# Mixer A's output products in another order: all products with the maps, then all with the states, the two heads in turn

## The chip, the cores and the metric

The kernel runs on one core of a Trainium2 chip. The time is the device time of one execution in microseconds (us). TensorE multiplies matrices and writes to PSUM, which has 8 banks of 512 fp32 columns over 128 partitions; VectorE, ScalarE and GpSimd do the element-wise work (GpSimd has no part in the copies out of PSUM here), and the DMA engines bring the weights.

## The reference, cut to what matters

Two blocks run one after the other: a block of two layers with four mixers each, side by side, then a second block with gating, convolutions, sparse attention and an MLP. The change is in mixer A of the first block, a gated linear recurrence in two directions over 512 latent and 256 context tokens, with four heads of 64 dimensions:

```python
# S_t = diag(f_t) S_{t-1} + k_t^T v_t ; o_t = q_t S_t, in chunks
o_inter = jnp.einsum('bthk,bhkv->bthv', qf * jnp.exp(bcum), s)
diff = bcum[:, :, None] - bcum[:, None, :]
decay = jnp.exp(jnp.where(incl[None, :, :, None, None], diff, -jnp.inf))
att = jnp.einsum('bthk,bshk,btshk->bhts', qf, kf, decay)
o_intra = jnp.einsum('bhts,bshv->bthv', att, vf)
```

The output of a chunk is the sum of a product with the chunk's own map (`o_intra`, in this kernel one map for both directions together) and of a product with the state that enters the chunk (`o_inter`), one for each direction. Everything is fp32.

## The kernel before, in words

The whole program is unrolled by Python. Activities are generators: "fillers" (the projections with weights, which come in a fixed list) and side chains (mixer A, the attentions, the norms). A planner runs them against estimated times, always takes the next activity whose inputs its estimate calls ready, and so writes the program's order. It also picks an engine for many copies, by the estimated time at which ScalarE, VectorE or GpSimd comes free (`best`, used by `cp` and `ts`). Behind it, the framework orders the instructions of each engine once more and sets the waits, so the order that runs can differ in places from the order written.

Mixer A is `j_a(pair)`, called by `chain_a` for the two pairs of heads of a layer, one after the other. Tokens stand in chunks of 128: six in layer 0 (with context, in parts of four and two, `aparts`), four in layer 1 (one part). For a pair, `j_a` builds the maps `att` in seven levels (`level_mm`, VectorE's predicated copies), transposes the keys, computes the update of each chunk and direction (tile `up`) and runs the recurrence over the chunks into the states `S` (tile `si`, VectorE; forward the last chunk's state is chunk 3's, backward chunk 0's).

The output products stand in the last loop of `j_a` (lines 1552 to 1566). For each part it takes two PSUM banks, `ps`. Head `j` of the pair (0 or 1) owns bank `j` and in it partitions 64j to 64j+63; chunk c of the part owns 128 columns. For each chunk and head there are three products into the same columns: values times map (`va`, `att`: 128 rows of the array, 64 columns, line 1560), and for each direction `d` state times queries (`S`, `QZ`: rows and columns 64j to 64j+63, so head 0 sits in one quarter of the array and head 1 in the opposite one, line 1562). The first of the three has `start=True`, the last `stop=True`. Then the two banks are copied to the tile `y` (shown as `hn` in the trace), half by half (line 1565), with `cp("*", ...)`, which picks the engine. Behind that stand the square, the head norm (`co_headnorm`) and the gate.

In the planner's estimate (`time`, line 550) a product with `va` costs 135 ns and one with `S` half of that, 67.5.

In the trace an fp32 product of this kind is two MATMUL records, each with a LDWEIGHTS record (engine PEld).

The softmax attentions end in products of the same shape as those with `va` (`seg_bd`: 128 rows, 64 columns, 128 queries, tile `bdv`), in which the two heads take turns.

Of the kernel before, what the change touches and what calls it, by code (L numbers as in the profile page):

```python
# [18 lines left out]
D, S, CL = 1024, 512, 256  # L19
# [438 lines left out]
class K:  # L458
# [1035 lines left out]
    def j_a(self, pair):  # L1494

        nc, M, P = self.nc, self.M, self.P
        nq = self.nq
        qs, F = self.fq.pop(pair)
        KZ, QZ, TZ = M.new([128, 2, NT], tag="kh"), M.new([128, 2, nq], tag="qh"), M.new([128, 2, NT], tag="T")
        att, ks = M.new([128, 2, nq], tag="att"), M.new([128, nq], tag="ks")  # L1500
        for d in range(2):
            self.ts("*", KZ[:, d], F[:, d], -1.0, 1.0, ALU.mult, ALU.add)
            self.mul("*", QZ[:, d], qs.f, F[:, d, :nq])
        self.add("*", ks.f, KZ[:, 0, :nq], KZ[:, 1, :nq])
        at = lambda z: lambda c: z[:, c * 128:(c + 1) * 128]
        for c0, n in self.aparts():
            yield (ks, qs, self.bank(2))
            self.level_mm(at(ks), at(qs), att, None, c0, n)
        M.free(ks, qs)
        for i in range(7):  # L1510
            h = 1 << i
            yield (KZ,)
            ks = M.new([128, nq], tag="ks")
            self.cp("*", ks.rearrange("p (b w h) -> p b w h", w=2, h=h), self.aview(KZ, False, h, 0, nq))
            for c0, n in self.aparts():
                yield (QZ, ks, self.bank(2))
                self.level_mm(at(ks), lambda c: self.aview(QZ, True, h, c * 128, 128), att, i, c0, n)
            M.free(ks)
            Tc, o = (F, 0) if i == 0 else (TZ, NT - 2 * (NT >> i))
            o2 = NT - 2 * (NT >> (i + 1))  # L1520
            nt = NT >> (i + 1)
            for z, flip, n in ((QZ, True, nq), (KZ, False, NT)):
                v = self.aview(z, flip, h, 0, n)
                self.mul("*", v, v, self.tview(Tc, flip, o, n // (2 * h), h))
            Tv = Tc[:, :, o:o + 2 * nt].rearrange("p d (b w) -> p d b w", w=2)
            self.mul("*", TZ[:, :, o2:o2 + nt], Tv[:, :, :, 0], Tv[:, :, :, 1])
        o = NT - 2 * (NT >> 7)
        S = M.new([128, 2, 6, 64], tag="si")
        for d in range(2):
            yield (KZ, self.bank(2))  # L1530
            ps = self.new_bank(2)
            for c in range(6):
                nc.tensor.transpose(ps[:, c * 128:(c + 1) * 128], KZ[:, d, c * 128:(c + 1) * 128], self.ident.f)
            self.cp("*", F[:, d], ps[:, :NT])
            P.free(ps)
        M.free(KZ)
        for d, order in ((0, (4, 5, 0, 1, 2, 3)), (1, (5, 4, 3, 2, 1, 0))):
            yield (F[:, d], self.bank())
            up = self.new_bank()
            for c in range(6):  # L1540
                for j in range(2):
                    hh = 2 * pair + j
                    nc.tensor.matmul(up[64 * j:64 * j + 64, c * 64:(c + 1) * 64], F[:, d, c * 128 + 64 * j:c * 128 + 64 * j + 64],
                                     self.va[:, c, hh * 64:hh * 64 + 64], start=True, stop=True)
            yield (up[:, 0:384],)
            nc.gpsimd.memset(S[:, d, order[0]], 0.0)
            for a, b in zip(order[:-1], order[1:]):
                self.stt(S[:, d, b], S[:, d, a], TZ[:, d, o + a:o + a + 1], up[:, a * 64:(a + 1) * 64], ALU.mult, ALU.add)
            P.free(up)
        M.free(F, TZ)  # L1550
        y = M.new([128, nq], tag="hn")
        for c0, n in self.aparts():
            yield (S, QZ, att, self.bank(2))
            ps = self.new_bank(2)
            for c in range(c0, c0 + n):
                for j in range(2):
                    hh, r = 2 * pair + j, slice(64 * j, 64 * j + 64)
                    cc = slice(c * 128, (c + 1) * 128)
                    out = ps[r, j * 512 + (c - c0) * 128:j * 512 + (c - c0 + 1) * 128]
                    nc.tensor.matmul(out, self.va[:, c, hh * 64:hh * 64 + 64], att[:, j, cc], start=True, stop=False)  # L1560
                    for d in range(2):
                        nc.tensor.matmul(out, S[r, d, c], QZ[r, d, cc], start=False, stop=d == 1)
            for j in range(2):
                r = slice(64 * j, 64 * j + 64)
                self.cp("*", y[r, c0 * 128:(c0 + n) * 128], ps[r, j * 512:j * 512 + n * 128])
            P.free(ps)
        M.free(S, QZ, att)
        if pair == 1:
            M.free(self.va)
        yield (y,)  # L1570
        q = M.new([128, nq], tag="hq")
        self.act(q.f, y.f, AF.Square)
        self.spawn("hn", self.co_headnorm(y, q, self.V(f"hg{self.l}"), pair, 4e-6), 0)
# [952 lines left out]
```

## Time and profile before

| | us |
|---|---|
| median of 3 runs (1985.46 to 1990.9) | 1987.78 |
| the profiled execution | 1988.87 |
| its span, first to last instruction | 1987.1 |
| TensorE busy in it | 1871.8 |
| VectorE, ScalarE, GpSimd busy | 1199.5, 623.6, 527.4 |

The profile is that of one execution. "Busy" is the time in which an engine had at least one instruction under way; matmuls are pipelined, so two of them that overlap count once, and a busy TensorE is not one at its peak. A group's row gives start, busy time and count; the time that a group occupies is read from its start to the next group's start. "Idle before <- X" is the engine's idle time ahead of the instruction and what ended it; "issue" is time in which it waited for nothing that the profile shows.

### The profile page before, as it was taken

Reading aid. Unit: us, or ns where it says so; the run is one execution under the profiler, and the core shown is the slowest. Engines: PE = TensorE matmul, PEld = TensorE weight load, DVE = VectorE, ACT = ScalarE, POOL = GpSimd, SP = SyncE. Lnnn points to the kernel's source line nnn. Section 1 sums busy time; section 2 is a strip of 40 time slices with the busy share of each in tenths; the row PEclk is TensorE's granted clock in tenths of the full one; section 3 lists DMA queues with packets and bytes.
Section 4 is the critical chain, followed back from the end, with each engine's and each line's share of the span. In section 5 each row is a group of like instructions: output and inputs, shape, how many; then the busy total and the mean of one; then the engine's idle time right before and its main releaser. Section 6 shows DMA issues by size and latency. Waiting matters only on the chain.

```text
span 1987.1 us, 28567 instructions
## 1 busy us (share of the span) xinstructions
PE 1871.8 (94%) x11446; PEld 1542.3 (78%) x11446; DVE 1199.5 (60%) x2053; ACT 623.6 (31%) x1277; POOL 527.4 (27%) x453
## 2 busy tenths in 40 slices
PE   6899999899999999899999989989999999999999
PEld 4688677688877787776787777878788778888887
DVE  2657774655657738766556978774533655545542
ACT  2345444334630135444435231244423211000100
POOL 1314332532222414533133354421211320000000
PEclk9999989999999999999999999999999999999999
DMA  9100410200132401002214231211223322232221
GB/s 355 54 22 30 150 56 30 79 23 22 56 114 94 146 11 44 22 12 96 65 59 145 93 104 64 67 51 51 93 88 111 106 75 85 96 126 78 72 96 64
DMA packets 45380, 159.22 MB, mean 80 GB/s; under 512 B 5040, under 2 KB 5552, under 8 KB 44992
## 3 DMA queue, kind: packets, MB, share of 16 engines
q1 hardware_dynamic: 42224, 148.54, 21.9%
q10 hardware_dynamic: 3024, 8.85, 1.3%
q8 instruction: 90, 1.47, 0.3%
q14 instruction: 42, 0.34, 0.1%
HBM read 152.12 MB, written 5.26 MB: 79 GB/s over the span
## 4 chain that ended last, share of the span: by engine, by line
PE 40%; DVE 13%; issue 4%; POOL 4%; ACT 1%; DMA 1%; ACTq 0%; POOLq 0%; DVEq 0%; SPq 0%
PE banks L282 40%; DVE cacc L282 3%; POOL t L282 2%; DVE t L282 1%; DVE wlo L282 1%; DVE sm L282 1%; DVE z L282 1%; DVE p L282 1%; DVE h L282 1%; ACT p L282 1%; DVE whi L282 0%; DVE gt L282 0%; DVE xr L282 0%; POOL p L282 0%; POOL qh L282 0%
## 5 line engine op out<-in xcount | busy, mean ns | idle before, releaser
L282 PE MATMUL banks<-h,whi 128*128 128x512 f32 (+1 forms) x1968 | 579.1, 378 | 6.2 <-ACT h L282 2.8
L282 PEld LDWEIGHTS banks<-h,whi 128*128 128x128 f32 x1968 | 351.7, 190 | 66.9 <-ACT h L282 3.3
L282 PE MATMUL banks<-h,wlo 128*128 128x512 f32 (+1 forms) x984 | 366.5, 372 | 0.0
L282 PE MATMUL banks<-whi,h 128*128 128x256 f32 (+3 forms) x1344 | 335.8, 332 | 15.9 <-DVE h L282 7.9
L282 DVE TENSOR_TENSOR wlo<-raw,whi 128x1024 fp32r<-128x1024 f32 (+2 forms) x175 | 222.6, 1275 | 106.2 <-PE banks L282 59.7
L282 PEld LDWEIGHTS banks<-whi,h 128*128 128x128 f32 x1344 | 234.7, 192 | 42.3 <-DVE h L282 9.8
L282 PE MATMUL banks<-wlo,h 128*128 128x256 f32 (+3 forms) x672 | 219.8, 328 | 7.1 <-DVE wlo L282 6.0
L282 POOL TENSOR_TENSOR wlo<-raw,whi 128x1024 fp32r<-128x1024 f32 (+2 forms) x41 | 104.0, 2540 | 456.5 <-DMA out<-z 299.7
L282 PEld LDWEIGHTS banks<-h,wlo 128*128 128x128 f32 x984 | 186.6, 190 | 32.7 <-DVE wlo L282 0.4
L282 DVE TENSOR_REDUCE sm<-banks 128x1 f32<-128x768 f32 (+5 forms) x192 | 140.0, 750 | 56.1 <-PE banks L282 53.2
L282 ACT ACTIVATE p<-banks,sm 128x768 f32<-128x768 f32 (+5 forms) x192 | 141.6, 741 | 95.0 <-DVE sm L282 84.2
L282 ACT CAST whi<-raw 128x1024 fp32r<-128x1024 f32 (+2 forms) x88 | 88.3, 1007 | 223.3 <-PE banks L282 147.4
L282 PE MATMUL banks<-whi,hid 128*128 128x512 f32 x512 | 157.9, 389 | 0.0
L282 DVE CAST whi<-raw 128x1024 fp32r<-128x1024 f32 (+2 forms) x103 | 73.2, 715 | 116.0 <-PE banks L282 98.0
L282 PEld LDWEIGHTS banks<-wlo,h 128*128 128x128 f32 x672 | 129.0, 192 | 18.2 <-DVE wlo L282 7.5
L282 PEld LDWEIGHTS banks<-whi,hid 128*128 128x128 f32 x512 | 96.1, 188 | 19.8
L282 PE MATMUL banks<-ident,p 128*128 128x128 f32 x656 | 98.3, 282 | 12.2 <-POOL p L282 2.7
L282 ACT COPY p<-banks 128x768 f32<-128x768 f32 (+5 forms) x118 | 73.6, 630 | 99.1 <-PE banks L282 96.3
L282 POOL TENSOR_TENSOR t<-t,mhalf 128x1 f32<-128x1 f32 (+5 forms) x51 | 65.3, 1283 | 142.3 <-DVE t L282 136.5
L282 PEld LDWEIGHTS banks<-ident,p 128*128 128x128 f32 x656 | 75.6, 144 | 32.7 <-issue 7.7
L282 PE MATMUL banks<-wlo,hid 128*128 128x512 f32 x256 | 99.6, 389 | 0.0
L282 ACT ACTIVATE rl<-banks 128x512 f32<-128x512 f32 (+1 forms) x35 | 19.7, 562 | 169.2 <-PE banks L282 169.2
(334 smaller groups left out, 3003.9 us busy)
## 6 DMA issues: line engine op xcount, KB each, us to landing
raw<-wm SPq DMA_DIRECT2D x64, 512.0 KB, 3.5
raw<-win SPq DMA_DIRECT2D x60, 512.0 KB, 3.6
raw<-wada SPq DMA_DIRECT2D x48, 512.0 KB, 4.1
raw<-wgate SPq DMA_DIRECT2D x32, 512.0 KB, 3.5
raw<-wout SPq DMA_DIRECT2D x24, 512.0 KB, 3.5
raw<-w2f SPq DMA_DIRECT2D x10, 512.0 KB, 3.5
xr<-xtok SPq DMA_DIRECT2D x6, 512.0 KB, 6.2
x<-z SPq DMA_DIRECT2D x6, 512.0 KB, 2.6
```

Of the source, the lines that this page charges most:

```text
L282: return f(*a, **kw)
```

## The change

The three products of a chunk and head no longer stand together. For a part, first all products with the maps are written, over chunks and in each chunk over the two heads; then all products with the forward states in the same order; then all with the backward states. So neighbouring products always belong to different heads. Since a bank's sums now stay open until the last direction, `start` is set only on the first chunk's map product of each bank, and `stop` only on the last chunk's backward product. Tiles, operands, copies and the number of products stay.

```diff
-            for c in range(c0, c0 + n):
-                for j in range(2):
-                    hh, r = 2 * pair + j, slice(64 * j, 64 * j + 64)
-                    cc = slice(c * 128, (c + 1) * 128)
-                    out = ps[r, j * 512 + (c - c0) * 128:j * 512 + (c - c0 + 1) * 128]
-                    nc.tensor.matmul(out, self.va[:, c, hh * 64:hh * 64 + 64], att[:, j, cc], start=True, stop=False)
-                    for d in range(2):
-                        nc.tensor.matmul(out, S[r, d, c], QZ[r, d, cc], start=False, stop=d == 1)
+            cj = [(c, slice(c * 128, (c + 1) * 128), j, slice(64 * j, 64 * j + 64)) for c in range(c0, c0 + n) for j in range(2)]
+            out = lambda c, j: ps[64 * j:64 * j + 64, j * 512 + (c - c0) * 128:j * 512 + (c - c0 + 1) * 128]
+            for c, cc, j, r in cj:
+                hh = 2 * pair + j
+                nc.tensor.matmul(out(c, j), self.va[:, c, hh * 64:hh * 64 + 64], att[:, j, cc], start=c == c0, stop=False)
+            for d in range(2):
+                for c, cc, j, r in cj:
+                    nc.tensor.matmul(out(c, j), S[r, d, c], QZ[r, d, cc], start=False, stop=d == 1 and c == c0 + n - 1)
```

## Rows read from the trace of the kernel before

**Rows 1.** The page: busy time by engine; the chain that ended last, by engine.

```profile
PE 1871.8 (94%) x11446; PEld 1542.3 (78%) x11446; DVE 1199.5 (60%) x2053; ACT 623.6 (31%) x1277; POOL 527.4 (27%) x453
...
PE 40%; DVE 13%; issue 4%; POOL 4%; ACT 1%; DMA 1%; ACTq 0%; POOLq 0%; DVEq 0%; SPq 0%
```

**Rows 2.** Product stretches: us, busy PE, PEld, DVE, ACT, POOL; PEclk, DMA share, GB/s.

```profile
295.75:306.82 11.07, 11.07 (x73) 6.95 (x72) 2.26 (x5) 1.35 (x3) 0.00 (x0) 1.00 0.05 22
...
423.33:434.61 11.28, 11.28 (x74) 7.16 (x73) 1.11 (x2) 1.62 (x4) 0.10 (x1) 1.00 0.01 2
...
885.88:893.40 7.52, 7.52 (x49) 4.78 (x48) 2.38 (x2) 0.58 (x1) 2.87 (x3) 1.00 0.25 72
...
958.43:968.07 9.64, 9.64 (x79) 6.41 (x78) 2.66 (x6) 0.58 (x1) 0.00 (x0) 1.00 0.06 23
```

**Rows 3.** Order of time, first stretch, the other engines: start, us, instruction, [idle before <-releaser].

```profile
303.73 0.58 ACT L282 COPY hn<-banks 64x512 f32<-64x512 f32 x1 [9.67 <-PE banks L282]
...
304.62 0.69 DVE L282 COPY hn<-banks 64x512 f32<-64x512 f32 x1 [7.48 <-PE banks L282]
...
306.84 0.74 POOL L282 TENSOR_TENSOR stg<-bd,stg 128x256 fp32r<-128x256 f32 x1 [17.32 <-ACT stg L282]
```

**Rows 4.** Order of time, first stretch: products with maps (att) and states (si).

```profile
296.47 0.27 DVE L282 SCALAR_TENSOR_TENSOR si<-si,T,banks 128x64 f32<-128x64 f32 x1
...
297.56 0.41 PEld L282 LDWEIGHTS banks<-qh,si 64*64 64x64 f32 x4 [0.17 <-issue]
297.56 0.65 PE L282 MATMUL banks<-qh,si 64*64 64x128 f32 x4
...
298.14 0.43 PE L282 MATMUL banks<-att,va 128*64 128x128 f32 x2
298.50 0.20 PEld L282 LDWEIGHTS banks<-qh,si 64*64 64x64 f32 x4 [0.17 <-issue]
298.50 0.43 PE L282 MATMUL banks<-qh,si 64*64 64x128 f32 x4
...
298.87 0.43 PE L282 MATMUL banks<-att,va 128*64 128x128 f32 x2
...
303.93 1.08 PE L282 MATMUL banks<-qh,si 64*64 64x128 f32 x8
...
304.94 0.43 PE L282 MATMUL banks<-att,va 128*64 128x128 f32 x2
```

**Rows 5.** Order of time, TensorE: a run with heads in turn; work inside the fourth stretch.

```profile
894.91 1.29 PEld L282 LDWEIGHTS banks<-p,bdv 128*64 128x64 f32 x24 [0.17 <-ACT p L282]
894.92 1.53 PE L282 MATMUL banks<-p,bdv 128*64 128x128 f32 x24
...
896.38 1.05 PE L282 MATMUL banks<-cst,hq 128*128 128x2 f32 x8
...
959.88 1.53 PE L282 MATMUL banks<-p,bdv 128*64 128x128 f32 x24
...
962.06 0.44 PE L282 MATMUL banks<-qh,si 64*64 64x128 f32 x4
```

**Rows 6.** Stretches between the products, and 780 to 840 us, columns as in rows 2.

```profile
306.82:423.33 116.51, 109.99 (x956) 91.26 (x955) 71.72 (x136) 49.33 (x102) 48.93 (x45) 0.97 0.15 51
...
434.61:885.88 451.27, 424.62 (x2887) 361.21 (x2886) 298.27 (x553) 181.16 (x390) 157.81 (x140) 0.99 0.17 57
...
893.40:958.43 65.03, 59.65 (x517) 44.42 (x516) 42.98 (x64) 31.66 (x53) 23.26 (x25) 0.95 0.29 95
...
968.07:1065.00 96.93, 95.71 (x709) 83.97 (x710) 56.62 (x115) 42.18 (x96) 29.71 (x31) 1.00 0.25 86
...
780.00:840.00 60.00, 51.88 (x403) 43.29 (x403) 47.19 (x66) 26.66 (x51) 34.80 (x29) 1.00 0.11 36
```

**Rows 7.** TensorE's waits behind the third and the first stretch: total, times, longest.

```profile
PE banks L282 <- POOL qh L282: 3.4, 1, 3.4
...
PE banks L282 <- DVE att L282: 2.6, 3, 1.8
```

## The prediction

> **What bounds the kernel now.** I read the page first. TensorE is busy for 94% of the span, and no other engine is over 60% but its own weight loads, which run beside it [rows 1]. So the first question about any TensorE change is whether the time it frees is time that TensorE would have been late by anyway. The chain of waits on the page puts only 40% of the span on TensorE and the rest on many [rows 1], so I don't take the answer from it but from stretches.
>
> The change touches four stretches, one for each pair of heads in each of the two layers. I cut the trace there [rows 2]: in all four TensorE is busy without a break, at the upper level of its clock (1.00, 2.4 GHz), while VectorE, ScalarE and GpSimd do next to nothing (over the first: 2.26, 1.35 and 0.00 of 11.07 us). The reader should see that these stretches are the opposite of an overlapped phase. The waits say the same: ScalarE and VectorE stand at the copy out of these very banks, 9.67 and 7.48 us at the first stretch, and GpSimd had been idle 17.32 us when it got its next work [rows 3]. Nobody has a backlog there that a shorter stretch would uncover.
>
> Inside the stretch the order of time shows the price [rows 4]. A product is two records (an fp32 product is run as two, each with its weight load). Two of the map records, then two or four of the state records, then map again, and at each change of form the weight loader shows 0.17 us put down to "issue". From start to start: 2 records of one form take 0.36 us (298.14 to 298.50), 4 records of one head take 0.58 (297.56 to 298.14), 8 take 1.01 (303.93 to 304.94). So one more record of the same head costs 0.108 us, and a change of form about 0.14 on top. One group differs: at 298.50 four state records take 0.37 us (to 298.87), and their four weight loads 0.20 instead of 0.41. There the order that ran was not the order written: the backward product of the first chunk had waited for its state (VectorE writes one at 296.47) and was put in later for both heads at once. Two heads' products, in opposite quarters of the array, took the time of one.
>
> The same kind of alternation in a long run is in the trace elsewhere [rows 5]: 24 records of the form 128*64, 128x128, the two heads in turn, take 1.46 us (894.92 to 896.38). That is 0.37 for the first four and (1.46 - 0.37)/20 = 0.0545 us for each further one, half of 0.108.
>
> **The change part by part.** It removes no product and adds none; it moves them.
>
> First, what the four stretches cost now. 11.07, 11.28 and 7.52 us [rows 2]; the fourth is 9.64 less the other work that stands in it, from 959.88 to 962.06, 2.18 us [rows 2, 5]: 7.46. Sum 37.3 us. Check: a chunk and head costs 0.36 + 0.58 = 0.94, and the second stretch has 12 of them: 11.28.
>
> Second, what they would cost. With the heads alternating, m records of one form take 0.37 + (m - 4) x 0.0545. A part of four chunks: 16 map records 1.02, 32 state records 1.90. A part of two chunks (layer 0 only): 8 map records 0.59, 16 state records 1.02. A pair in layer 0: 4.53 us, in layer 1: 2.92; two of each: 14.9. TensorE saves 37.3 - 14.9 = **22.4 us**. Of this, the changes of form fall from 24 to 4 for a pair of layer 0 and from 16 to 2 in layer 1, by 68 in all at 0.14, or 9.5 us; the rest is the alternation.
>
> Two prices in it are not shown for the very form. For the map phase the nearest row is the 24-record run of the same shape [rows 5], so I take it as it stands; the other end is 0.108 a record. For the state phase (64*64) the only row with two heads is the group of four at 298.50 [rows 4]; in a long run it could be as dear as 0.108, or cheaper than 0.0545 if the quarters also overlap with what follows. I take 0.0545, because in that group the second head's two records came for nothing, so two heads cost 0.109 for two records each. At 0.108 the state phases would cost 8.5 us more.
>
> On weight loads the row shows 24 of them in 1.29 us in the run whose heads share all 128 rows of the array and differ in columns [rows 5]. The Trainium skill, page "TensorE: Matmul & The Clock Gate", Part 3, states that a weight load overlaps with running matmuls only when the row group differs. By that, the map phase, whose heads share the rows, would gain nothing from alternating; the trace disagrees, with 0.061 us a record over the run, and I keep the row.
>
> The flag "start" moves to the first chunk alone. It is a field of an instruction and costs nothing; what it could cost is a wait between products, and products of one engine show none here [rows 4]. The products of the backward state come last now, 1.02 + 0.96 us into a part; VectorE wrote the first stretch's last state 0.7 us into it (296.47) [rows 4], so the wait for it is gone there. Where it isn't, as in the fourth stretch, into whose products other work was put [rows 5], TensorE could wait for it a second time, some 1 us in all.
>
> The copies out of the banks start sooner: the first head's copy now needs nearly the last product of its part, but that comes some 5 us earlier (295.75 + 1.02 + 1.90 against a copy that starts at 303.73 [rows 3]). Behind these copies on ScalarE and VectorE stand the square, the norm and the weight splits, and those gain the same. No DMA moves; buffers come free earlier, and the DMA engines are busy 1 to 29% in the stretches and between them [rows 2, 6].
>
> **How much of 22.4 arrives.** Between the first stretch and 1065 us, outside the products, TensorE is busy 689.97 of 729.74 us [rows 6], idle 39.8, or 5.4%. What it waits for there is mostly VectorE and GpSimd work on mixer A and the softmaxes, 3.4 us at the longest behind the third stretch and 1.8 behind the first [rows 7]. These engines wait for TensorE in turn [rows 3], so most of their work shifts with it. Bounds: none is lost, or half is (the first waits behind a stretch swallow it). I take one tenth lost, about twice the idle share, nearer the lower bound because of the starved engines [rows 3]. 22.4 x 0.9 = 20.2 us. From 1065 us on everything hangs on layer 1's end and shifts as it is.
>
> The profiled execution took 1988.87 us (span 1987.1 and 1.8 around it): 1988.87 - 20.2 = 1968.7. It lies 1.1 us above the median of 1987.78, so against the median **1967.6 us**.
>
> **The rivals.**
> 1. Given back downstream: half of the gain is swallowed by the waits of [rows 7], because pair 1's levels run at GpSimd's pace (the 3.4 us wait for qh is such a place). For it: 8.3% idle after the third stretch (5.38 of 65.03 us). Against: 1.3% after the fourth (1.22 of 96.93) [rows 6]. 1987.8 - 11.2 = 1976.6.
> 2. The state phase stays serial, 0.108 a record. For it: only two four-record groups show two heads at once [rows 4, 5]. Saved 13.9, times 0.9: 1975.3.
> 3. The map phase stays serial (0.108), by the mechanism that a weight load has to wait for the matmul in its rows: 4.2 us less saved, 18.2 x 0.9: 1971.4. This is the result of the skill's rule above; [rows 5] speak against it.
> 4. It doesn't do what it says: the order that runs is not the order written (298.50 [rows 4]), and forms could be mixed again, with other work between. At half the saving 1977.7, at none 1987.8.
> 5. Slower: the planner. It writes the order of all work from estimated times. In its estimate the first head's last product comes 202 ns later than now (67.5 instead of 270 ns before the end), so its copy on ScalarE ends later, and a choice of engine or of the next step behind it can flip and re-order what follows. The place is TensorE's idle time of 39.8 us; the change loses when that grows by over 20.2, to a share of 8.2%. If half of the 729.74 us ran at the 13.5% idle of 780 to 840 us [rows 6] and half as now, idle is 69: 1967.6 + 29 = 1997. Against: the estimated end of the part and of the last copy stay the same.
>
> **How the numbers follow.** Forecast (1961 to 1973) 0.55; rival 1 0.14; rival 2 0.10; rival 3 0.04; rival 4 0.11; rival 5 0.06. The low end of the range is all of 22.4 and a tenth of the idle time, 4 us, won as well, with 1 us of scatter: 1960. The high end takes in rivals 1 to 3 and half of rival 4: 1981.5. A measurement tells 0.3%, 6 us, from no change. Faster by more: forecast, rivals 2 and 3, most of 1 and a part of 4: 0.83. Within: the rest of 1 and 4: 0.11. Slower: rival 5, 0.06.
>
> **What would show it.** In the order of time: groups of 16 map and 32 state records (8 and 16 for the second part of layer 0), 1.0 and 1.9 us long, with 0.17 "issue" only between them; stretches of 4.5 and 2.9 us; ScalarE's wait for the first copy near 5 instead of 9.7 us. State groups near 3.6 us mean rival 2, map groups near 1.9 rival 3. TensorE's busy sum falls by 22. Idle time from 307 to 1065 that grows by as much as that means rival 1, another order of work outside the stretches rivals 4 or 5. The prediction is wrong if TensorE's sum falls and the span doesn't follow.

## The result, and the profile after

The changed kernel takes 1963.61 us, the median of 4 runs (1959.76 to 1970.03), against 1987.5 for the kernel before beside it (four runs): a ratio of 0.9882 with a 95% interval of 0.9867 to 0.9897, or 23.9 us less. A second group of runs, beside another set of runs of the kernel before, gave 1965.89 us and 0.9888 (0.9874 to 0.9903). The forecast was 1967.6 in a range of 1960 to 1981.5.

The profiled execution of the changed kernel was the longest of its four: 1970.03 us (1968.3 of it the span), with a mean granted clock of 0.976, where the other three had 0.980, 0.982 and 0.983 at 1964.54, 1962.67 and 1959.76 us. So a comparison of the two traces shows 18.8 us of span where the medians show 23.9; the difference is looked at in the last section.

The page's first line, against [rows 1]: TensorE's busy sum is down by 15.3 us, the others have hardly moved.

```profile
PE 1856.5 (94%) x11446; PEld 1539.2 (78%) x11446; DVE 1204.4 (61%) x2055; ACT 622.7 (32%) x1275; POOL 522.9 (27%) x453
```

The stretches of products and the stretches between them, with the columns of [rows 2] and [rows 6]:

```profile
296.22:300.75 4.53, 4.53 (x74) 3.84 (x73) 2.68 (x6) 1.26 (x3) 0.42 (x1) 1.00 0.11 43
300.75:416.40 115.65, 108.85 (x956) 91.05 (x955) 74.84 (x138) 48.81 (x102) 48.85 (x46) 0.99 0.16 51
416.40:423.16 6.76, 6.76 (x74) 5.73 (x73) 1.38 (x3) 1.22 (x3) 0.73 (x1) 1.00 0.00 0
423.16:877.91 454.75, 430.70 (x2888) 367.32 (x2886) 299.02 (x552) 182.09 (x389) 151.23 (x139) 0.97 0.17 57
877.91:880.83 2.92, 2.92 (x49) 2.57 (x48) 2.38 (x2) 0.00 (x0) 2.83 (x3) 1.00 0.62 185
880.83:945.85 65.02, 59.76 (x518) 44.54 (x516) 42.98 (x64) 32.12 (x54) 23.21 (x26) 0.95 0.29 94
945.85:949.72 3.87, 3.87 (x60) 3.18 (x59) 2.67 (x6) 0.00 (x0) 0.00 (x0) 1.00 0.17 70
949.72:1046.35 96.63, 96.49 (x719) 84.60 (x717) 55.75 (x115) 42.36 (x97) 28.52 (x31) 1.00 0.26 85
```

The four stretches are 4.53, 6.76, 2.92 and 3.07 us long (the fourth is 3.87 less 0.80 of softmax products that stand in it, from 947.90 to 948.70): 17.27 in all, where they were 37.3. So 20.05 us are gone from them. Between and behind them TensorE is idle 6.80 + 5.26 + 24.05 + 0.14 = 36.25 us (length less busy PE of the other four rows); before it was 39.8 [rows 6].

The first stretch in order of time (start, length, engine, line, operation, count, and in brackets the idle time before and what ended it), against [rows 3, 4]:

```profile
296.22 0.85 PEld L282 LDWEIGHTS banks<-att,va 128*64 128x64 f32 x16 [0.17 <-issue]
296.22 1.09 PE L282 MATMUL banks<-att,va 128*64 128x128 f32 x16
...
297.24 1.72 PEld L282 LDWEIGHTS banks<-qh,si 64*64 64x64 f32 x32 [0.17 <-issue]
297.25 1.96 PE L282 MATMUL banks<-qh,si 64*64 64x128 f32 x32
299.14 0.42 PEld L282 LDWEIGHTS banks<-att,va 128*64 128x64 f32 x8 [0.17 <-issue]
299.14 0.66 PE L282 MATMUL banks<-att,va 128*64 128x128 f32 x8
299.28 0.69 DVE L282 COPY hn<-banks 64x512 f32<-64x512 f32 x1 [1.68 <-PE banks L282]
299.30 0.58 ACT L282 COPY hn<-banks 64x512 f32<-64x512 f32 x1 [4.77 <-PE banks L282]
299.73 0.85 PEld L282 LDWEIGHTS banks<-qh,si 64*64 64x64 f32 x16 [0.17 <-issue]
299.73 1.09 PE L282 MATMUL banks<-qh,si 64*64 64x128 f32 x16
...
300.33 0.72 POOL L282 TENSOR_TENSOR stg<-bd,stg 128x256 fp32r<-128x256 f32 x1 [10.30 <-ACT stg L282]
```

From start to start: 16 map records 1.03 us, 32 state records 1.89, 8 map records 0.59, 16 state records 1.02. The weight loader's 0.17 us of "issue" stands four times, at each change of form, instead of at every change within each chunk. The copies start at 299.28 and 299.30 instead of 304.62 and 303.73, though the stretch began 0.47 us later, and ScalarE's wait ahead of its copy is 4.77 instead of 9.67 us. GpSimd's idle time before its next work is 10.30 instead of 17.32: these engines were starved, and they moved up with TensorE.

The second stretch of the changed kernel looks different:

```profile
416.40 1.09 PE L282 MATMUL banks<-att,va 128*64 128x128 f32 x8
417.42 1.08 PE L282 MATMUL banks<-qh,si 64*64 64x128 f32 x8
418.43 1.31 PE L282 MATMUL banks<-att,va 128*64 128x128 f32 x10
419.67 1.96 PE L282 MATMUL banks<-qh,si 64*64 64x128 f32 x24
421.56 0.65 PE L282 MATMUL banks<-att,va 128*64 128x128 f32 x6
422.14 1.09 PE L282 MATMUL banks<-qh,si 64*64 64x128 f32 x16
423.16 1.53 PE L282 MATMUL banks<-p,bdv 128*64 128x128 f32 x24
```

The program's map products were written for the two heads in turn. What ran is 8 map records of one head, then its state records, and the other head behind them. The first 8 map records take 1.02 us here, where 16 took 1.03 above. In the instruction order that was built, four map products and four state products of head 1 stand ahead of the first product of head 0. By the built program, head 1's bank held a product that VectorE casts to `qs`, head 0's the chunk updates that VectorE's last state updates read, and the cast stands ahead of those:

```profile
415.09 0.42 DVE L282 CAST qs<-banks 128x256 fp32r<-128x256 f32 x1
...
415.43 0.90 DVE L282 SCALAR_TENSOR_TENSOR si<-si,T,banks 128x64 f32<-128x64 f32 x3
```

As I read it, the builder, which puts instructions in order by what is ready in its own estimate, therefore took head 1's products first. By the trace the last of these state updates had ended at 416.33, before the stretch began at 416.40, so head 0's products need not have come later.

### The profile page after: what moved, and what is told of

Its sections match the earlier page's. It is cut to its first block, busy times and chain, and to the rows that moved or that the text cites. A ratio compares the mean times of both kernels' runs of the same rounds, so it can differ in the third digit from the quotient of the medians.

```text
span 1968.3 us, 28571 instructions
## 1 busy us (share of the span) xinstructions
PE 1856.5 (94%) x11446; PEld 1539.2 (78%) x11446; DVE 1204.4 (61%) x2055; ACT 622.7 (32%) x1275; POOL 522.9 (27%) x453
## 3 DMA queue, kind: packets, MB, share of 16 engines
HBM read 152.12 MB, written 5.26 MB: 80 GB/s over the span
## 4 chain that ended last, share of the span: by engine, by line
PE 42%; DVE 12%; POOL 4%; issue 3%; ACT 2%; DMA 1%; ACTq 0%; POOLq 0%; DVEq 0%; SPq 0%
PE banks L282 42%; DVE cacc L282 3%; POOL t L282 2%; DVE t L282 1%; DVE wlo L282 1%; DVE z L282 1%; DVE sm L282 1%; DVE h L282 1%; DVE p L282 1%; ACT p L282 1%; DVE xr L282 0%; DVE whi L282 0%; DVE gt L282 0%; POOL wlo L282 0%; DVE xn L282 0%
```

## The experiments

In the kernel an order of products is used twice: the planner runs its estimate over it, and the instructions are issued in it. In most of the kernels below the loop of the output products is written so that the two are given separately (a product is a triple of chunk c, head j and d; d = -1 is the map, 0 and 1 are the states):

```python
C, H = range(c0, c0 + n), range(2)
OLD   = [(c, j, d) for c in C for j in H for d in (-1, 0, 1)]
NEW   = [(c, j, d) for d in (-1, 0, 1) for c in C for j in H]
CHUNK = [(c, j, d) for c in C for d in (-1, 0, 1) for j in H]
HEAD  = [(c, j, d) for ds in ((-1,), (0, 1)) for j in H for d in ds for c in C]
for c, j, d in EST:                       # the planner's estimate
    self.time("P", "matmul", ...)
for c, j, d in ISSUE:                     # what TensorE gets
    nc.tensor.real.matmul(out, a, b, start=first of the bank, stop=last of the bank)
```

With EST = OLD all other work is laid out as in the kernel before. In the traces these products then bear line 1570 or 1571. "Stretches" is the sum of the four product stretches in a kernel's trace, other work taken out, and is 37.32 for the kernel before and 17.27 for the changed one.

### The new issue order alone, under the old plan

```diff
+EST = OLD
+ISSUE = NEW
```

> The products are issued in the changed order, but the planner's estimate is fed in the old order, so everything else is written as in the kernel before. Theory (the products' own time is the gain): the four stretches shrink from 37.3 to 14.9 us (4.53 and 2.92 for a pair), and nine tenths or more of 22.4 arrive: 1965 to 1968. Rival (the changed kernel's 23.9 us are in part the luck of another plan, since its stretches sum to 17.3, not 14.9): here the gain is no more than 20 us although the stretches are shorter than in the changed kernel.

Measured: 1966.04 us, ratio 0.9882 (0.9866 to 0.9899), stretches 15.04. In another group, beside the by-head order (below), the same kernel:

> Old plan, changed order, once more, to be set beside the run without turns on this chip: 15.0 us in the stretches, ratio to the kernel before 0.988.

Measured: 1965.19 us, ratio 0.9883 (0.9869 to 0.9896), stretches 15.04. All that the prediction's sum asked of the stretches is there, 22.3 us, and about 23 arrive; the rival (no more than 20) is out. The second stretch of the first of these kernels, where the changed kernel went out of turn:

```profile
417.80 1.09 PE L1570 MATMUL banks<-att,va 128*64 128x128 f32 x16
418.82 1.96 PE L1570 MATMUL banks<-qh,si 64*64 64x128 f32 x32
420.72 0.66 PE L1570 MATMUL banks<-att,va 128*64 128x128 f32 x8
421.30 1.09 PE L1570 MATMUL banks<-qh,si 64*64 64x128 f32 x16
```

From 417.80 to the next work at 422.32 are 4.52 us.

### The new plan alone, with the old issue order

```diff
+EST = NEW
+ISSUE = OLD
```

> The products are issued in the old order (maps and states in turn, one head at a time), but the planner's estimate is fed in the changed order, so everything else is written as in the changed kernel. Theory: the plan alone is worth nothing, the stretches stay at 37 us and the time within 0.2% of the kernel before (1984 to 1991). Rival (luck of the plan): 3 to 5 us faster, the part of 23.9 that the products' 20.0 don't explain; or slower by a few us, when the new plan costs something that the products paid for.

Measured: 1984.54 us, ratio 0.9977 (0.9968 to 0.9986), stretches 36.88. The products are nearly as dear as before, and the kernel is still 4.6 us faster, with an interval of 1.8 each way: the theory (the plan alone is worth nothing) is a miss, and the rival's 3 to 5 us came. Nothing but the estimate of a few products was changed, by some tenths of a microsecond, and work elsewhere stands in another order. Two views show it in the order of time of VectorE, around the second stretch: first the old plan (the kernel of the flag alone, below), then the new plan.

```profile
417.44 2.38 DVE L282 SCALAR_TENSOR_TENSOR si<-si,T,banks 128x64 f32<-128x64 f32 x8
419.98 0.42 DVE L282 CAST qs<-banks 128x256 fp32r<-128x256 f32 x1 [0.15 <-PE banks L282]
```

```profile
417.13 1.88 DVE L282 SCALAR_TENSOR_TENSOR si<-si,T,banks 128x64 f32<-128x64 f32 x6 [0.54 <-PE banks L282]
418.93 0.69 DVE L282 CAST whi<-raw 128x1024 fp32r<-128x1024 f32 x1
419.53 0.28 DVE L282 SCALAR_TENSOR_TENSOR si<-si,T,banks 128x64 f32<-128x64 f32 x1
```

Under the new plan a weight split has gone in between VectorE's state updates.

Not all of the 4.6 us need be the order of work. The ten executions ran at a mean granted clock of 0.9815, the 14 of the kernel before beside them at 0.9794, and among the 41 executions of the kernel before in the three groups of runs the time is shorter by about 1 us for each 0.001 of it (an estimate: 0.8, 1.0 and 1.0 by group). So about 2 of the 4.6 us go with the clock; whether the plan raised it or chance did is not shown. For the other 2.5 the traces have places. The second stretch is 10.84 us long instead of 11.28, since its order moved as well, and between the second and the third stretch TensorE is idle for 23.54 us (length less busy PE) where it was 25.83 in the kernel of the flag alone (columns as in [rows 2], that kernel first):

```profile
432.57:887.17 454.60, 428.77 (x2887) 365.17 (x2886) 298.82 (x553) 181.35 (x390) 156.95 (x140) 0.98 0.17 57
...
431.92:883.75 451.83, 428.29 (x2887) 364.76 (x2886) 297.82 (x552) 181.86 (x388) 152.40 (x139) 0.98 0.17 57
```

Which of the moved steps does it is not shown.

### The flag alone

```diff
+EST = OLD
+ISSUE = OLD
-start=True at each map product
+start=True at the first product of a bank, stop=True at its last
```

> Old plan and old order of the products, but the sums are left open across the bank as in the change: start on the first product of a bank alone, stop on its last. Theory: the flags cost nothing, the stretches stay at 37.3 us and the time within 0.15% of the kernel before. It also shows how far two runs of one and the same order of work differ.

Measured: 1988.52 us, ratio 1.0003 (0.9995 to 1.0012), stretches 37.32. A sum that is left open across the bank costs nothing and brings nothing. It also shows that the way these kernels are written changes nothing by itself.

### The turns without the phases

```diff
+EST = OLD
+ISSUE = CHUNK
```

> Old plan; the heads take turns inside each chunk (both maps, both forward states, both backward states), but maps and states still alternate from chunk to chunk. Theory by its two terms: a chunk is 4 map records (0.37 us) and 8 state records (0.59), 0.96 instead of 1.88; the stretches sum to 19.2 us, 18.1 less than before, and the time is 1968 to 1972. If the change of form were the larger part of the gain, the stretches would stay near 28 us and the time near 1978.

Measured: 1968.45 us, ratio 0.9898 (0.9885 to 0.9912), stretches 19.43. The heads take turns, but each chunk still changes its form. In order of time, in the third stretch:

```profile
872.50 0.44 PE L1570 MATMUL banks<-att,va 128*64 128x128 f32 x4
872.87 0.65 PE L1570 MATMUL banks<-qh,si 64*64 64x128 f32 x8
873.45 0.44 PE L1570 MATMUL banks<-att,va 128*64 128x128 f32 x4
```

4 map records take 0.37 and 8 state records 0.58 us, 0.95 a chunk of two heads where it was 1.88. This order saves 17.9 of the 22.3 us. It is not the turns alone: as both heads now share a group, the groups of one form fall from 80 to 40 as well, by the order written (12 in the new order).

### The phases without the turns

```diff
+EST = OLD
+ISSUE = HEAD
```

> Old plan; all maps first and then all states, as in the change, but in each phase first all products of one head, then all of the other, so neighbours share a head. Theory: the changes of form go, the turns don't come: 16 map records 1.9 us, 32 state records 3.6, stretches 8.3 and 5.5 us a pair, sum 27.6, 9.7 us less than before; time 1977 to 1980. If the phases alone did it, the stretches would be 4.5 and 2.9 us and the time near 1966.

Measured: 1969.02 us, ratio 0.9904 (0.9889 to 0.992), stretches 23.02; this is a miss, both in the stretches, where 27.6 stood, and in the time, where 1977 to 1980 stood. A second time, in one group with the new order:

> Old plan, phases without turns, once more on the chip of the next run. Its stretches are 23.0 us, 8.0 more than with turns. Theory: 6 to 9 us above the run with turns. Rival: within 3 us of it, as in the first pair.

Measured: 1971.36 us, ratio 0.9921 (0.9908 to 0.9935), stretches 23.02; 6.2 us behind the new order of the same group for 8.0 us in the stretches, within the 6 to 9 expected, where the first pair of runs had 3.0. In order of time, the third stretch:

```profile
874.06 1.58 PE L1570 MATMUL banks<-att,va 128*64 128x128 f32 x16
875.57 3.32 PE L1570 MATMUL banks<-qh,si 64*64 64x128 f32 x32
878.82 0.44 PE L282 MATMUL banks<-ident,p 128*128 128x128 f32 x2
```

The 16 map records take 1.51 us and the 32 state records 3.25; in turns they take 1.02 and 1.89, and at 0.108 a record and 0.14 for the change of form they would take 1.87 and 3.60. Each phase is 0.36 us shorter than that because the second head's records begin while those of the first are not done: its first map record starts at 874.55, after 0.49 us, when five of the first head's eight have started, so that the last three of the one run beside the first of the other. In the single records the starts of a head lie 0.109 us apart, 0.160 behind the first, and from 874.55 on a second series with the same spacing stands between the first head's. The order that the builder made has all products of the first head ahead of the second's, so it is TensorE that begins them early.

### The changed kernel with its products held in the written order

```diff
-nc.tensor.matmul(out(c, j), ...)
+keep_in_program_order(nc.tensor.matmul(out(c, j), ...))
```

> The changed kernel, its products pinned to the order written, so that the second stretch (6.76 us there, because the framework put eight records of one head first) comes to 4.5 as well; all else runs in the changed kernel's order. Theory: the stretches sum to 15.0 us instead of 17.3 and the time is some 2 us below the changed kernel's (1961 to 1964 against a kernel before at 1988). If the 2.2 us went nowhere, the time equals the changed kernel's.

In the same group, the changed kernel once more:

> The changed kernel once more, beside the other runs of this chip: ratio to the kernel before 0.988 as before, stretches 17.3 us. It is the reference for the run with the pinned order, and shows with its second profile how far the granted clock in the stretches between the products moves the time of one and the same program.

Measured: 1962.18 us, ratio 0.9873 (0.9861 to 0.9886), stretches 15.13 with the order held; 1965.89 us, ratio 0.9888 (0.9874 to 0.9903), stretches 17.27 for the changed kernel. The second stretch is 4.68 us long instead of 6.76, with groups of 16, 32, 8 and 16 records; one softmax record of 0.06 us stands behind the first of its map records:

```profile
414.59 1.09 PE L282 MATMUL banks<-att,va 128*64 128x128 f32 x15
415.61 1.96 PE L282 MATMUL banks<-qh,si 64*64 64x128 f32 x32
417.50 0.66 PE L282 MATMUL banks<-att,va 128*64 128x128 f32 x8
418.09 1.09 PE L282 MATMUL banks<-qh,si 64*64 64x128 f32 x16
```

This is the fastest kernel of the study. The two intervals overlap, so that the 2.1 us of stretch time is shown in the trace, and in the time only as a lower median by 3.7 us.

### What a microsecond in the stretches is worth

Two kernels issue each output product a second time (the whole order is repeated for a part, before its copies, and the second pass begins each bank anew), so that they do the work of the products twice:

```diff
+EST = OLD
+ISSUE = NEW, each pass issued twice
```

> Old plan, changed order, and every output product is issued a second time (the second pass starts the banks anew, so the sums stay the same). It adds 15.0 us to TensorE and nothing else. Theory (TensorE's time in these stretches is paid in full or nearly, nine tenths or more): 13 to 15 us above the run with old plan and changed order (1966), so 1979 to 1981. Rival (other engines bound the stretches behind them, so that only half of a change arrives): 1973 to 1975.

Measured: 1980.62 us, ratio 0.9962 (0.9948 to 0.9976), stretches 29.93.

```diff
+EST = OLD
+ISSUE = HEAD, each pass issued twice
```

> Old plan, phases without turns (one head, then the other), every product issued a second time. The stretches sum to about 46 us (twice 23.0), 16 more than the same with turns (29.9). Theory (each us of these stretches is a us at the end, turns included): 8.7 us above the kernel before, so 1995 to 1999, and 14 to 18 above the doubled order with turns (1980.6). Rival (the time that turns save goes nowhere, as the single by-head run at 1969 beside 1966 hints): within 8 us of 1980.6.

Measured: 1996.5 us, ratio 1.0041 (1.0029 to 1.0054), stretches 46.29. The first of the two passes in its third stretch, in order of time:

```profile
889.88 1.58 PE L1571 MATMUL banks<-att,va 128*64 128x128 f32 x16
891.39 3.32 PE L1571 MATMUL banks<-qh,si 64*64 64x128 f32 x32
```

Both came as the theory had it. Doubling the new order adds 14.9 us to the stretches and 0.9962 - 0.9882 = 0.0080 of 1988 us, 15.9 us (4.3 each way by the two intervals), to the time. The two doubled kernels differ in nothing but the turns, by 16.4 us in the stretches and by 1.0041 - 0.9962 = 0.0079, 15.7 us (3.7 each way), in the time. All kernels under the old plan, by their stretches; the times come from three groups of runs, so the ratios are what to compare:

| issue order | stretches, us | time, us | ratio |
|---|---|---|---|
| by head, twice | 46.3 | 1996.5 | 1.0041 |
| old | 37.3 | 1988.5 | 1.0003 |
| new, twice | 29.9 | 1980.6 | 0.9962 |
| by head | 23.0 | 1969.0 and 1971.4 | 0.9904 and 0.9921 |
| turns in a chunk | 19.4 | 1968.5 | 0.9898 |
| new | 15.0 | 1966.0 and 1965.2 | 0.9882 and 0.9883 |

From the first to the last row it is 31.3 us in the stretches and 0.0158 to 0.0159, some 31.5 us, in the time: one microsecond for one. A straight line through all 87 executions behind this table, the kernels before included and each group of runs with its own level, has a slope of 1.07 us of time for one of stretch, 0.06 each way by their scatter; nine tenths is outside. Under that line the by-head order lies by 3.8 us in its first group and by 0.4 in its second. In the first its executions ran at a mean granted clock of 0.9816 and the kernel before beside them at 0.9794 (0.9798 and 0.9793 in the second); by the 1 us for 0.001 estimated above that is 2.2 of the 3.8, and the rest is within the interval of 3.1 us each way. So the time that turns save does arrive, and the 3.0 us between the first pair of runs were largely the clock.

## Why the prediction was right

**The price of the products held.** It was read from a few rows of a trace in which only one short group and one run of another tile had the heads in turn [rows 4, 5], and it came out to a hundredth: 1.02 us for 16 map records, 1.89 for 32 state records against 1.90, 0.59 and 1.02 for 8 and 16. The two prices without a row of their own were both at the value taken. Rival 2, state records at 0.108 each, would have shown 3.6 us for 32. Rival 3, the map phase at 0.108 because both heads' weights go into the same rows, would have shown 1.87 us; with turns it is 1.02, and without them, by head, 1.51. So the rule of the Trainium skill that was weighed there ("TensorE: Matmul & The Clock Gate", Part 3), read as the prediction read it, doesn't hold for these products, which share the rows and differ in columns.

**Two effects, as counted.** The sum put 9.5 us on the changes of form and the rest of 22.4, 12.9, on the turns. No run has the one without any of the other, but both mixed orders come out of these two prices. Turns inside a chunk also halve the groups of one form, 40 of 80 gone at 0.14: 12.9 + 5.6 = 18.5 us, and 17.9 were measured. Phases by head also bring the overlap where one head's records meet the other's, 13 phases in the trace (one of 12 is split by other work) at 0.36: 9.5 + 4.7 = 14.2, and 14.3 were measured. That is why the two savings make more than the 22.3 us of both together. The overlap where the heads meet is what the expectation of the by-head order lacked.

**Mis-sized by 2.3 us: what the stretches save.** 20.05 instead of 22.4, because the second stretch took 6.76 us instead of 4.53. This is rival 4, in one of four places: the order that runs was not the order written. Held in the written order, the same program has 4.68 us there. The prediction had the sign of this risk in its own row, the group at 298.50 that had been moved [rows 4], and gave the whole rival 0.11 without a term in the sum.

**Mis-sized by one tenth: how much arrives.** The prediction took 0.9. The doubled kernels show 15.9 us of time for 14.9 of stretch and 15.7 for 16.4, and the line through all executions 1.07, so all of it arrives. The idle time between the stretches, which was to grow if the gain were given back (rival 1), fell from 39.8 to 36.25 us. The fall is the plan's: in the nine traces with the old plan it is 37.6 to 39.8 us whatever the issue order, in the four with the new plan 35.9 to 36.3. The turns left it as it was. TensorE's waits behind the stretches stand at nearly the same length (the columns are total, times, longest; first behind the third, then behind the first):

```profile
PE banks L282 <- POOL qh L282: 3.4, 1, 3.4
...
PE banks L282 <- DVE att L282: 2.5, 3, 1.8
```

against 3.4 and 2.6 [rows 7]. At the first stretch the other engines were themselves waiting for it to end [rows 3], so, as I read it, their work moved up by the same time and the waits stayed as they were. That reason was in the prediction, and the tenth taken off for caution had nothing behind it but the idle share.

**Rival 5's mechanism came, with the other sign.** The planner's estimate shifted and work from the second stretch on stands in another order. It was priced as a loss; the new plan alone, with the old products, measures as a gain of 4.6 us (1.8 each way), of which about 2 go with a higher granted clock. That it could be a gain was in the low end of the range, as a tenth of the idle time, but in no forecast.

**The sum.** The forecast had 20.2 us; 23.9 were measured. Its two errors on the stretches, 2.3 us less saved and a tenth more arriving, are of one size and cancel, which is luck. The 3.7 us by which it was too slow are of the size of the plan's gain under the old issue order, but the runs don't show that gain on top of the new order: the changed kernel and the new order under the old plan have the same ratio, 0.9882, while their stretches differ by 2.2 us, and with the written order held under the new plan it is 0.9873 against 0.9882, inside the intervals. So the turns and phases explain the gain to within the scatter, and how much of the rest is plan, clock or chance stays open.

**The flag** costs nothing, as the prediction had it (1.0003, 0.9995 to 1.0012).

## What to carry to other kernels

In a stretch where TensorE alone works, neighbours in its order should sit in different halves or quarters of the array and have the same form; here that made 37.3 us of small fp32 products into 15, without one product less. What it brings can be read ahead from the starts of neighbouring groups in the trace, for one form in turn, one form not in turn, and a change of form, and it is worth its full length if the waits around it show the other engines standing idle for the result. Then look in the trace whether the order written is the order that runs, and separate what a new order does to TensorE from what it does to a planner's estimate: here the shifted estimate alone, under the old issue order, moved the time by 4.6 us, and under the new order it put one stretch out of turn. Set the granted clocks of two sets of runs beside each other before a difference of a few microseconds is explained.

## What the runs showed that was not expected

- TensorE runs one head's products beside the end of another's even when they are not written in turn: in the by-head order the second head's first map record started when five of the first head's eight had started, and a phase was 0.36 us shorter for it. The reach is short, though: about three records in every phase, and 1.51 us for 16 map records that take 1.02 in turns.
- The same program differs from execution to execution by the granted clock. The new order under the old plan has two profiled executions: 1969.9 us with a mean granted clock of 0.976, and 1960.07 with 0.982. TensorE's busy sum was 1854.2 us in the first and 1848.4 in the second, so some 5.8 of the 9.8 us are the same instructions at a lower clock, and the other 4.0 are idle time of TensorE. One such place, by stretches (columns as in [rows 2]) and in order of time, in the first execution:

```profile
347.00:353.00 6.00, 3.99 (x42) 3.16 (x40) 4.57 (x7) 2.17 (x3) 2.34 (x3) 1.00 0.04 16
353.00:360.00 7.00, 6.03 (x24) 3.22 (x25) 3.16 (x4) 0.83 (x2) 4.84 (x2) 0.51 0.09 13
...
353.97 2.82 PE L282 MATMUL banks<-ident,p 128*128 128x128 f32 x12 [1.78 <-DVE att L282]
```

and the same work in the second:

```profile
342.00:348.00 6.00, 4.07 (x42) 3.23 (x41) 4.50 (x7) 2.11 (x4) 2.35 (x3) 1.00 0.10 41
348.00:355.00 7.00, 5.97 (x50) 3.57 (x52) 3.23 (x4) 1.70 (x3) 4.96 (x2) 1.00 0.23 78
...
349.03 1.56 PE L282 MATMUL banks<-ident,p 128*128 128x128 f32 x12 [1.78 <-DVE att L282]
```

Ahead of it TensorE had been as busy in the one as in the other, 3.99 and 4.07 of 6 us, and then waited the same 1.78 us for VectorE. Behind that the clock was at its lower level (0.51, near 1.2 GHz) in the first and at the upper (1.00, 2.4 GHz) in the second, and the same twelve matmuls took 2.82 and 1.56 us. So a stretch with gaps can lose its clock in one execution and keep it in the next. Such places are why the changed kernel's profiled execution shows only 15.3 us less of TensorE's work, where the stretches alone are 20 us shorter and the prediction's sign was 22: from 423.16 to 877.91 its clock is 0.97, against 0.99 before, and TensorE is busy for 430.70 us instead of 424.62 [rows 6]. What decides between the two is not shown by these runs.
